# A step of a hybrid transformer layer on one core: x transposed by token tile in the opening, and adaLN slabs in other places

## The chip, the core and the metric

The kernel runs on one core of one Trainium2 chip. A core has TensorE (PE; its weight loads are shown apart as PEld), VectorE (DVE), ScalarE (ACT), GpSimd (POOL) and SyncE (SP), which issues most of the transfers from DRAM. The metric is the device time of one execution in microseconds (us), the median of several runs.

## The reference

One layer of a flow-matching backbone on 384 tokens (128 context tokens, 256 latent ones), width 2048, all in float32. What bears on the change is its beginning:

```python
mod = silu(cond) @ ada_w + ada_b          # cond: c_ctx for the context, c for the latents; 6 parts of 2048
h = rmsnorm(x, norm_w[0]) * (1 + scale_a) + shift_a
proj = h @ w_in                           # q, k, v, o, gates, u
```

Of `mod` the first two parts, shift and scale (i = 0 and 1 in the kernel), are needed for h. Behind it come a bidirectional mLSTM over 8 heads, a pooling mixer on u, an output projection and a squared-ReLU MLP of width 8192; they are the greater part of the time and the change leaves them alone.

## The kernel before, in words

Float32 products are made of three matmuls: an operand is split into `hi` (ACT rounds it to fp32r) and `lo` (DVE subtracts), and hi*hi + lo*hi + hi*lo is summed in PSUM. `load_w` (L119 to L136) fetches a block of weights to `raw` (three buffers) and splits it so.

The opening has four threads. **x**: three token tiles `x_tok` of 128 x 2048 are loaded; ACT sums their squares (L389) for the RMS norm's rstd `rx`, which a matmul spreads over all partitions (`bc_rx`, copied to `rbc`). `transpose_x(k)` (L400) takes the k-th 128 columns of all three token tiles into one PSUM bank and copies them, 128 x 384 at a time, to `xT[k]`; even k on DVE, odd k on ACT. **adaLN**: the columns of `ada_w` for one pair of k tiles come in slabs of 512 KB (four for shift, four for scale), and four matmuls a slab (L257, eight in the profile, since each is recorded twice) sum them in a bank. `ada_rows` copies that bank to SBUF (`ada_sb`, ACT, L269), turns it with small matmuls (L273), and `ada_finish` (L281, L286) writes `mod`. **h**: `make_h(s)` (L437) makes h for one pair of k tiles: `hm` = xT * scale * rbc on DVE (four operations, L443), `hh` = hi of hm + shift on ACT (L448), `hl` on DVE (L449). **Weights** of u and v, in five chunks per k pair: u 0, u 512, v 0, v 3 and v 6 (with the gates); written below as u, u_512, v0, v3, v6.

`X_ORDER` sets by letters how transposes (t), adaLN steps (a) and the row of rstd (b) follow each other. The main loop (L491) then goes over eight k pairs and five chunks, with three token tiles each; between chunks it takes steps of the adaLN generator `ada0` for the next pair: in the first pair by `ADA_STEPS`, after that by a fixed rule. `load_ahead` issues the weights of coming chunks. In the first part the order on PE, DVE and ACT is as written; in the main loop PE's is as written, and a scheduler set that of DVE and ACT ahead of time. All three run strictly in their order, as does SP's queue.

Slabs go into four buffers of their own (`adap`, tag ada) and into four spare places: the second halves of the three x tiles, which are u's tiles later, and the masks (`spare`, L433).

## Time and profile before

| | us |
|---|---|
| median of 3 runs | 1685.16 |
| the runs | 1682.71 to 1686.5 |
| the profiled execution | 1684.17 |
| its span | 1682.5 |
| PE busy in the span | 1654.3 (98%) |
| DVE busy | 1340.3 (80%) |
| ACT busy | 751.3 (45%) |

Times in the views count from the start of the span. In a timeline row stand start, length, engine, line, operation, out<-in, shape and count, and in brackets the idle time before it and what ended it. In the chain of waits stand start, length and what the end of the program waited for in that time. In a row by stretch stand the stretch and its length, then for PE, PEld, DVE, ACT and POOL the busy time and the number of instructions, then the granted clock of PE, the busy share of the DMA engines and GB/s. PE's matmuls overlap: their records are longer than the distance from one start to the next.

### The profile page before, as it was taken

Reading aid. Unit: us, or ns where it says so; the run is one execution under the profiler, and the core shown is the slowest. Engines: PE = TensorE matmul, PEld = TensorE weight load, DVE = VectorE, ACT = ScalarE, POOL = GpSimd, SP = SyncE. Lnnn points to the kernel's source line nnn. Section 1 sums busy time; section 2 is a strip of 40 time slices with the busy share of each in tenths; the row PEclk is TensorE's granted clock in tenths of the full one; section 3 lists DMA queues with packets and bytes.
Section 4 is the critical chain, followed back from the end, with each engine's and each line's share of the span. In section 5 each row is a group of like instructions: output and inputs, shape, how many; then the busy total and the mean of one; then the engine's idle time right before and its main releaser. Section 6 shows DMA issues by size and latency. Waiting matters only on the chain.

```text
span 1682.5 us, 27870 instructions
## 1 busy us (share of the span) xinstructions
PE 1654.3 (98%) x10965; PEld 1581.4 (94%) x10965; DVE 1340.3 (80%) x2009; ACT 751.3 (45%) x1225; POOL 133.3 (8%) x185
## 2 busy tenths in 40 slices
PE   6999999999999999999999999999999999999997
PEld 3888999999999989989999999999999999999996
DVE  3677769898999959997897688988588588588688
ACT  5322355555443345543444444444444444445443
POOL 1000002221000024520000000000000000000120
PEclk9999999999999999999999999999999999999999
DMA  9999757786789954754546246444344443443653
GB/s 318 332 310 298 253 172 248 240 258 221 238 273 311 311 194 142 209 151 128 178 154 195 84 135 187 152 144 150 101 151 129 123 138 118 145 124 113 186 182 136
DMA packets 258099, 320.95 MB, mean 191 GB/s; under 512 B 14784, under 2 KB 223120, under 8 KB 257584
## 3 DMA queue, kind: packets, MB, share of 16 engines
q1 hardware_dynamic: 250688, 303.62, 57.1%
q0 software_dynamic: 5984, 13.78, 2.9%
q8 instruction: 86, 1.41, 0.4%
q10 hardware_dynamic: 1296, 1.77, 0.3%
q14 instruction: 45, 0.37, 0.1%
HBM read 308.61 MB, written 10.51 MB: 190 GB/s over the span
## 4 chain that ended last, share of the span: by engine, by line
PE 94%; DVE 3%; issue 1%; DMA 1%; ACT 0%; SPq 0%; POOL 0%; DVEq 0%; ACTq 0%; POOLq 0%
PE acc_w L145 10%; PE acc_w L144 10%; PE acc_w L146 10%; PE v L503 4%; PE y L1231 4%; PE y L1232 4%; PE y L1230 4%; PE u L503 4%; PE acc_wo L144 3%; PE acc_wo L145 3%; PE acc_wo L146 2%; PE y_yz L1231 2%; PE y_yz L1230 2%; PE y_yz L1232 2%; PE y L1074 2%; PE y L1073 2%
## 5 line engine op out<-in xcount | busy, mean ns | idle before, releaser
L145 PE MATMUL acc_w<-h2l,hi_w 128*128 128x384 f32 (+1 forms) x1024 | 346.2, 338 | 0.5 <-DVE h2l L1024 0.5
L144 PE MATMUL acc_w<-h2h,hi_w 128*128 128x384 f32 (+1 forms) x1024 | 344.2, 338 | 1.2 <-ACT h2h L1020 1.2
L146 PE MATMUL acc_w<-h2h,lo_w 128*128 128x384 f32 (+1 forms) x1024 | 345.1, 337 | 0.0
L136 DVE TENSOR_TENSOR lo_w<-raw_w,hi_w 128x1024 fp32r<-128x1024 f32 x152 | 185.3, 1220 | 136.5 <-ACT hi_w L135 136.3
L135 ACT ACTIVATE hi_w<-raw_w 128x1024 fp32r<-128x1024 f32 x152 | 160.8, 1058 | 213.7 <-PE acc_w L145 83.4
L317 DVE SCALAR_TENSOR_TENSOR ada_acc<-ada_raw,sg,ada_acc 128x1024 f32<-128x1024 f32 (+1 forms) x240 | 252.0, 1081 | 2.1 <-DMA ada_raw<-in_ada_w_dram 2.1
L144 PEld LDWEIGHTS acc_w<-h2h,hi_w 128*128 128x128 f32 x1024 | 192.2, 188 | 2.9 <-ACT h2h L1020 2.0
L145 PEld LDWEIGHTS acc_w<-h2l,hi_w 128*128 128x128 f32 x1024 | 192.6, 188 | 1.2 <-DVE h2l L1024 0.8
L146 PEld LDWEIGHTS acc_w<-h2h,lo_w 128*128 128x128 f32 x1024 | 192.4, 188 | 0.3 <-DVE lo_w L136 0.2
L1216 ACT ACTIVATE hi_t<-w 128x1024 fp32r<-128x1024 f32 x104 | 109.5, 1059 | 118.7 <-PE y L1232 34.0
L1217 DVE TENSOR_TENSOR lo_t<-w,hi_t 128x1024 fp32r<-128x1024 f32 x104 | 126.3, 1220 | 15.1 <-ACT hi_t L1216 14.7
L1217 DVE TENSOR_TENSOR lo_b<-w,hi_b 128x1024 fp32r<-128x1024 f32 x78 | 95.3, 1221 | 40.0 <-ACT hi_b L1216 39.8
L1216 ACT ACTIVATE hi_b<-w 128x1024 fp32r<-128x1024 f32 x78 | 82.5, 1060 | 97.0 <-PE acc_w L145 64.6
L135 ACT ACTIVATE hi_wo<-raw_wo 128x1024 fp32r<-128x1024 f32 x32 | 34.0, 1064 | 81.3 <-DMA raw_wo<-in_w_out_dram 64.0
L950 ACT ACTIVATE z<-acc_w 128x384 f32<-128x384 f32 x54 | 26.3, 487 | 74.8 <-PE acc_w L146 74.8
L503 PE MATMUL v<-hi_v,hh 128*128 128x384 f32 (+1 forms) x144 | 47.8, 332 | 0.0
L503 PE MATMUL v<-lo_v,hh 128*128 128x384 f32 (+1 forms) x144 | 46.5, 323 | 0.0
L503 PE MATMUL v<-hi_v,hl 128*128 128x384 f32 (+1 forms) x144 | 46.5, 323 | 0.0
L136 DVE TENSOR_TENSOR lo_wo<-raw_wo,hi_wo 128x1024 fp32r<-128x1024 f32 x32 | 38.8, 1218 | 7.3 <-ACT hi_wo L135 6.3
L986 POOL DMA_DIRECT2D gf_dram<-gfT x1 | 0.5, 521 | 551.9 <-DVE gfT L985 551.9
L144 PE MATMUL acc_k<-hh,hi_k 128*128 128x384 f32 x128 | 44.2, 345 | 0.0
L144 PE MATMUL acc_o<-hh,hi_o 128*128 128x384 f32 x128 | 43.9, 343 | 0.0
(2268 smaller groups left out, 4566.9 us busy)
## 6 DMA issues: line engine op xcount, KB each, us to landing
raw_w<-in_w_dram SPq DMA_DIRECT2D x152, 512.0 KB, 4.3
ada_raw<-in_ada_w_dram SPq DMA_DIRECT2D x130, 512.0 KB, 5.0
w<-in_w_dram SPq DMA_DIRECT2D x104, 512.0 KB, 4.4
raw_wo<-in_w_out_dram SPq DMA_DIRECT2D x32, 512.0 KB, 5.6
u<-in_ada_w_dram SPq DMA_DIRECT2D x18, 512.0 KB, 6.0
raw_u<-in_w_in_dram SPq DMA_DIRECT2D x16, 512.0 KB, 7.0
raw_q<-in_w_in_dram SPq DMA_DIRECT2D x16, 512.0 KB, 4.7
raw_k<-in_w_in_dram SPq DMA_DIRECT2D x16, 512.0 KB, 4.7
```

The costliest lines, as they stand in the source:

```text
L135: nc.scalar.activation(hi[:, 0:n], raw[:, 0:n], AF.Copy)
L136: low = lambda: nc.vector.tensor_tensor(lo[:, 0:n], raw[:, 0:n], hi[:, 0:n].bitcast(F32), op=ALU.subtract)
L144: nc.tensor.matmul(ps, lh, rh, start=start, stop=False)
L145: nc.tensor.matmul(ps, lh, rl, start=False, stop=False)
L146: mm3.ins = nc.tensor.matmul(ps, ll, rh, start=False, stop=stop).ins
L317: nc.vector.scalar_tensor_tensor(acc[:, g, :], raw[:, a, :], cj, acc[:, g, :], op0=ALU.mult, op1=ALU.add)
L503: nc.tensor.matmul(acc[i][:, 0:n], h[k0 + k][a][:, i * P:(i + 1) * P], (hi, lo)[b][:, k, :], start=k == 0 and a + b == 0, stop=k == nk - 1 ...
L1216: nc.scalar.activation(hi, raw, AF.Copy)
L1217: nc.vector.tensor_tensor(lo, raw, hi.bitcast(F32), op=ALU.subtract)
L1230: nc.tensor.matmul(acc, xh, wh, start=start and j == 0, stop=False)
L1231: nc.tensor.matmul(acc, xh, wl, start=False, stop=False)
L1232: nc.tensor.matmul(acc, xl, wh, start=False, stop=stop and j == 3)
```

## The change

x is transposed by token tile. `transpose_x(i, k0, on_act)` takes four k tiles of one token tile into a bank, and the copies are 128 x 128, four a bank, on DVE or ACT by a flag; all `xT` tiles are allocated ahead. x_prompt is the first load on SP; the constants are loaded from ACT's queue. Two banks of the context tile and one bank of each latent tile are transposed as the tiles land; a list `x_rest` of eight more banks is worked off at the x's of the new `X_ORDER` and in `shift_rows`, so that no transposes are left behind u. u's first weights are loaded in two halves (one per k tile) with a rounding each, `hi_first`, which `make_h(0)` calls ahead of each k tile's hh.

In the first k pair `ADA_STEPS` moves the adaLN steps: the first four slabs from behind u to behind u_512, the second four from behind v0 to behind v3. These second four now go into the spare places, and in the later pairs the first four slabs use the `adap` buffers and the last four the spare ones. The small matmuls and `make_h(1)` move from the middle of v3 into v6, behind its first three matmuls. `AHEAD` sets how far weights are issued ahead in the first pair.

```diff
@@ -28,9 +28,9 @@
 N_E = 1
-XT_AT = 0
-ADA_STEPS = (4, 0, 4, 0, 0)
-X_ORDER = "tatatatattaatabata"
+ADA_STEPS = (0, 4, 0, 4, 0)
+AHEAD = (1, 1, 3, 2, 3)
+X_ORDER = "aaxabaxaaxaxaxax"
 N_X = 4
@@ -77,15 +77,16 @@
     masks = vp.tile([P, N_CST - 3, P], F32, name="masks")
-    nc.sync.dma_start(cc[:, 0, :], c_ctx.rearrange("(p j) -> p j", j=16))
-    nc.sync.dma_start(cc[:, 1, :], c[0].rearrange("(p j) -> p j", j=16))
-    nc.sync.dma_start(cst[:, 0:3], cs_src[:, 0:3])
+    nc.scalar.dma_start(cst[:, 0:3], cs_src[:, 0:3])
...
     x_tok = [pre.tile([P, D], F32, tag=f"x{i}", name=f"xtok{i}") for i in range(3)]
-    for t, src in zip(x_tok, (x_prompt[0], x_sample[0, 0:128], x_sample[0, 128:256])):
-        nc.sync.dma_start(t, src)
+    nc.sync.dma_start(x_tok[0], x_prompt[0])
+    nc.sync.dma_start(cc[:, 0, :], c_ctx.rearrange("(p j) -> p j", j=16))
+    nc.sync.dma_start(cc[:, 1, :], c[0].rearrange("(p j) -> p j", j=16))
+    for i in (1, 2):
+        nc.sync.dma_start(x_tok[i], x_sample[0, (i - 1) * P:i * P])
     nc.gpsimd.dma_start(prm[0:96, 1, :], ada_b[0].rearrange("(r p) -> r p", p=P))
@@ -237,7 +238,7 @@
-    def ada_mat(parts, tags=("ada",), raws=None):
+    def ada_mat(parts, tags=("ada",), raws=None, into=()):
@@ -249,7 +250,8 @@
                 if raw is None:
-                    raw = (wp if tag == "lo" else adap).tile([P, nj, w], F32, tag=tag, name=f"ada_raw_{i}_{k0}_{j0}", bufs=N_W if tag == "lo" else N_ADA)
+                    raw = (into[b][j0 // nj] if into else
+                           (wp if tag == "lo" else adap).tile([P, nj, w], F32, tag=tag, name=f"ada_raw_{i}_{k0}_{j0}", bufs=N_W if tag == "lo" else N_ADA))
                     nc.sync.dma_start(raw, aw[:, j0:j0 + nj, c0:c0 + w])
@@ -348,7 +350,8 @@
             elif k0 == 2:
-                yield from ada_mat([(0, k0, nk), (1, k0, nk)])
+                some = [adap.tile([P, 4, 256], F32, tag="ada", name=f"ada_raw_0_{k0}_{j}", bufs=N_ADA) for j in range(0, 16, 4)]
+                yield from ada_mat([(0, k0, nk), (1, k0, nk)], into=(some, spare))
             else:
@@ -359,9 +362,9 @@
                 i, j0 = divmod(4 * len(raws), 16)
-                raw = (spare.pop(0) if len(raws) < 4 else
+                raw = (spare.pop(0) if len(raws) >= 4 else
                        adap.tile([P, 4, 256], F32, tag="ada", name=f"ada_raw_{i}_{k0}_{j0}", bufs=N_ADA))
-                if len(raws) < 4:
+                if len(raws) >= 4:
                     spare.append(raw)
@@ -375,51 +378,59 @@
     ada0 = first_ada()
+    ssq = const.tile([P, 3, 2], F32, name="ssq")
+    junk = wp.tile([P, 1024], F32, tag="hi", name="junk", bufs=N_W)
+    rx = const.tile([P, 3], F32, name="rx")
+    ss = const.tile([P, 3], F32, name="ss")
+    xT_dram = dram.tile([P, KT, NTOK], F32, name="xT_dram")
+    xT = [slot(f"xT{k}") for k in range(KT)]
+    rbc = pre.tile([P, NTOK], F32, name="rbc")
+    def squares(i):
+        for q in range(2):
+            nc.scalar.activation(junk, x_tok[i][:, q * 1024:(q + 1) * 1024], AF.Square, accum_out=ssq[:, i, q:q + 1])
+    xt_late = []
+    def transpose_x(i, k0, on_act, later=False):
+        ps = bank(f"xt_{i}_{k0}")
+        for a in range(4):
+            nc.tensor.transpose(ps[:, a * P:(a + 1) * P], x_tok[i][:, (k0 + a) * P:(k0 + a + 1) * P], ident)
+        def copy():
+            for a in range(4):
+                dst, src = xT[k0 + a][:, i * P:(i + 1) * P], ps[:, a * P:(a + 1) * P]
+                if on_act:
+                    nc.scalar.activation(dst, src, AF.Copy)
+                else:
+                    nc.vector.tensor_copy(dst, src)
+        if later:
+            xt_late.append(copy)
+        else:
+            copy()
+    squares(0)
+    for q in range(2):
+        transpose_x(0, 4 * q, False)
     pp = bank("pp")
...
     nc.vector.tensor_copy(prmT[:, 0:80], pp[:, 96:176])
-    ssq = const.tile([P, 3, 2], F32, name="ssq")
-    junk = wp.tile([P, 1024], F32, tag="hi", name="junk", bufs=N_W)
-    rx = const.tile([P, 3], F32, name="rx")
-    for i in (0, 1, 2):
-        for q in range(2):
-            nc.scalar.activation(junk, x_tok[i][:, q * 1024:(q + 1) * 1024], AF.Square, accum_out=ssq[:, i, q:q + 1])
-    xT_dram = dram.tile([P, KT, NTOK], F32, name="xT_dram")
-    xT = []
-    rbc = pre.tile([P, NTOK], F32, name="rbc")
-    ss = const.tile([P, 3], F32, name="ss")
+    squares(1)
+    transpose_x(1, 0, False)
+    squares(2)
+    transpose_x(2, 0, False)
     nc.vector.tensor_reduce(ss, ssq, axis=AX.X, op=ALU.add)
     rstd_cols(rx, ss, 3, 1.0 / D)
-    xt_late = []
-    def transpose_x(k, later=False):
-        ps = bank(f"xt_{k}")
-        for i in range(3):
-            nc.tensor.transpose(ps[:, i * P:(i + 1) * P], x_tok[i][:, k * P:(k + 1) * P], ident)
-        t = slot(f"xT{k}")
-        xT.append(t)
-        def copy():
-            if k % 2:
-                nc.scalar.activation(t[:, 0:NTOK], ps[:, 0:NTOK], AF.Copy)
-            else:
-                nc.vector.tensor_copy(t[:, 0:NTOK], ps[:, 0:NTOK])
-        if later:
-            xt_late.append(copy)
-        else:
-            copy()
+    x_rest = [(1, 4, False), (1, 8, True), (1, 12, True), (2, 4, False), (2, 8, False), (2, 12, False), (0, 8, False, True), (0, 12, True, True)]
     for op in X_ORDER:
-        if op == "t":
-            transpose_x(len(xT))
-        elif op == "a":
+        if op == "a":
             next(ada0)
+        elif op == "x":
+            transpose_x(*x_rest.pop(0))
         else:
@@ -443,7 +454,9 @@
             between()
-        for k, t, hi, lo in ts:
+        for n, (k, t, hi, lo) in enumerate(ts):
+            if s == 0:
+                hi_first[n]()
             for g, (a, b) in enumerate(GROUPS):
@@ -462,8 +475,12 @@
-    lo_later = []
-    loaded = {0: load_chunk(0, 0, later=lo_later)}
+    raw0 = wp.tile([P, 2, 512], F32, tag="raw", name="raw_u_first", bufs=3)
+    hi0, lo0 = (wp.tile([P, 2, 512], F32R, tag=t, name=f"{t}_u_first", bufs=N_W) for t in ("hi", "lo"))
+    for k in range(2):
+        nc.sync.dma_start(raw0[:, k, :], wv_in[:, k, U0:U0 + 512])
+    hi_first = [lambda k=k: nc.scalar.activation(hi0[:, k, :], raw0[:, k, :], AF.Copy) for k in range(2)]
+    loaded = {0: (hi0, lo0, 512)}
@@ -475,14 +492,12 @@
     def shift_rows():
-        for _ in range(2):
-            transpose_x(len(xT), True)
         next(ada0)
-        for _ in range(2):
-            transpose_x(len(xT), True)
+        while x_rest:
+            transpose_x(*x_rest.pop(0))
     h_ins = make_h(0, shift_rows)
-    lo_later[0]()
+    nc.vector.tensor_tensor(lo0, raw0, hi0.bitcast(F32), op=ALU.subtract)
     for copy in xt_late:
@@ -491,7 +506,7 @@
             k0, nk = ksteps[s]
-            load_ahead(5 * s + ci, 1 if s + ci == 0 else N_AHEAD)
+            load_ahead(5 * s + ci, AHEAD[ci] if s == 0 else N_AHEAD)
             hi, lo, n = loaded.pop(5 * s + ci)
@@ -502,16 +517,17 @@
                                              start=k == 0 and a + b == 0, stop=k == nk - 1 and b == 1)
-                    if ci == 3 and k == 0:
+                        if s == i == k == 0 and ci == 4:
+                            with tc.high_priority():
+                                next(ada0)
+                                make_h(1)
+                    if s > 0 and ci == 3 and k == 0:
                         next(ada0, None)
...
                 load_ahead(1, 1)
-            if s == 0 and ci == XT_AT:
-                while len(xT) < KT:
-                    transpose_x(len(xT))
             for _ in range((ADA_STEPS if s == 0 else (1, 1, 1, 0, 0))[ci]):
                 next(ada0, None)
-            if ci == 3 and s < NS - 1:
+            if ci == 3 and 0 < s < NS - 1:
                 make_h(s + 1)
...
```

Names below carry the program's buffer numbers; the lines are those of the kernel before, and of the changed one.

DVE ahead of u's first matmuls, before (xT6 is a transposed k tile, `mod` in L281 the shift):

```order
L411 COPY xT6_217<-xt_6_213 128x384
L207 TENSOR_TENSOR dg_rx_225<-cst_72,rx_126 128x384
L424 COPY rbc_134<-bc_rx_227 128x384
L443 SCALAR_TENSOR_TENSOR hm0_261<-xT0_143,mod_118,rbc_134 128x128
L443 SCALAR_TENSOR_TENSOR hm0_261<-xT0_143,mod_118,rbc_134 128x256
L443 SCALAR_TENSOR_TENSOR hm1_266<-xT1_156,mod_118,rbc_134 128x128
L443 SCALAR_TENSOR_TENSOR hm1_266<-xT1_156,mod_118,rbc_134 128x256
L281 TENSOR_TENSOR mod_118<-ada_0_0_206,prmT_117 128x4
L449 SCALAR_TENSOR_TENSOR hl0_263<-hm0_261,mod_118,hh0_262 128x128
```

The same place in the changed kernel:

```order
L406 COPY xT12_136<-xt_2_12_299 128x128
L406 COPY xT13_137<-xt_2_12_299 128x128
L406 COPY xT14_138<-xt_2_12_299 128x128
L406 COPY xT15_139<-xt_2_12_299 128x128
L454 SCALAR_TENSOR_TENSOR hm0_319<-xT0_124,mod_118,rbc_140 128x128
L454 SCALAR_TENSOR_TENSOR hm0_319<-xT0_124,mod_118,rbc_140 128x256
L454 SCALAR_TENSOR_TENSOR hm1_324<-xT1_125,mod_118,rbc_140 128x128
L454 SCALAR_TENSOR_TENSOR hm1_324<-xT1_125,mod_118,rbc_140 128x256
L283 TENSOR_TENSOR mod_118<-ada_0_0_245,prmT_117 128x4
L462 SCALAR_TENSOR_TENSOR hl0_321<-hm0_319,mod_118,hh0_320 128x128
```

The four copies of token tile 2's last bank now stand ahead of hm; the rstd row's operations stand further up.

PE at the end of the first k pair, before:

```order
L257 MATMUL ada_0_2_361<-ada_raw_1_2_8_465,cT_109 32x256 x4
L257 MATMUL ada_0_2_361<-ada_raw_1_2_12_471,cT_109 32x256 x4
L503 MATMUL v_3_0_0_488<-hi_v_3_0_397,hh0_262 128x384
L503 MATMUL v_3_0_0_488<-hi_v_3_0_397,hl0_263 128x384
L503 MATMUL v_3_0_0_488<-lo_v_3_0_398,hh0_262 128x384
L503 MATMUL v_3_0_1_489<-hi_v_3_0_397,hh0_262 128x384
L503 MATMUL v_3_0_1_489<-hi_v_3_0_397,hl0_263 128x384
L503 MATMUL v_3_0_1_489<-lo_v_3_0_398,hh0_262 128x384
L503 MATMUL v_3_0_2_490<-hi_v_3_0_397,hh0_262 128x384
L503 MATMUL v_3_0_2_490<-hi_v_3_0_397,hl0_263 128x384
L503 MATMUL v_3_0_2_490<-lo_v_3_0_398,hh0_262 128x384
L273 MATMUL ada_0_2_361<-cst_72,ada_sb_0_2_477 128x4 x2
```

and in the change, where the slabs lie in u's tiles and the masks:

```order
L518 MATMUL v_3_0_2_488<-hi_v_3_0_451,hl1_326 128x384
L518 MATMUL v_3_0_2_488<-lo_v_3_0_452,hh1_325 128x384
L259 MATMUL ada_0_2_419<-u0_308,cT_109 32x256 x4
L259 MATMUL ada_0_2_419<-u1_309,cT_109 32x256 x4
L259 MATMUL ada_0_2_419<-u2_310,cT_109 32x256 x4
L259 MATMUL ada_0_2_419<-masks_81,cT_109 32x256 x4
L518 MATMUL v_6_0_0_544<-hi_v_6_0_458,hh0_320 128x288
L518 MATMUL v_6_0_0_544<-hi_v_6_0_458,hl0_321 128x288
L518 MATMUL v_6_0_0_544<-lo_v_6_0_459,hh0_320 128x288
L275 MATMUL ada_0_2_419<-cst_72,ada_sb_0_2_527 128x4 x2
L518 MATMUL v_6_0_1_545<-hi_v_6_0_458,hh0_320 128x288
```

The second four slabs' matmuls moved from ahead of v3 to behind it, and the small matmuls from the middle of v3 to the fourth place in v6.

ACT at the same place, before:

```order
L269 ACTIVATE ada_sb_0_2_477<-ada_0_2_361 128x256
L135 ACTIVATE hi_u_0_1_484<-raw_u_0_1_482 128x1024
L522 ACTIVATE v0_85<-v_3_0_0_488 128x3x128
L135 ACTIVATE hi_u_512_1_537<-raw_u_512_1_535 128x1024
L522 ACTIVATE v1_86<-v_3_0_1_489 128x3x128
L448 ACTIVATE hh2_515<-hm2_514,mod_118 128x128
L448 ACTIVATE hh2_515<-hm2_514,mod_118 128x256
L448 ACTIVATE hh3_520<-hm3_519,mod_118 128x128
L448 ACTIVATE hh3_520<-hm3_519,mod_118 128x256
L522 ACTIVATE v2_87<-v_3_0_2_490 128x3x128
L522 ACTIVATE v0_85<-v_6_0_0_541 128x2x128
L522 ACTIVATE v1_86<-v_6_0_1_542 128x2x128
```

and in the change:

```order
L136 ACTIVATE hi_u_0_1_534<-raw_u_0_1_532 128x1024
L538 ACTIVATE v2_85<-v_3_0_2_488 128x3x128
L136 ACTIVATE hi_u_512_1_540<-raw_u_512_1_538 128x1024
L271 ACTIVATE ada_sb_0_2_527<-ada_0_2_419 128x256
L136 ACTIVATE hi_v_0_1_596<-raw_v_0_1_594 128x768
L538 ACTIVATE v0_83<-v_6_0_0_544 128x2x128
L538 ACTIVATE v1_84<-v_6_0_1_545 128x2x128
L538 ACTIVATE v2_85<-v_6_0_2_546 128x2x128
L461 ACTIVATE hh2_556<-hm2_555,mod_118 128x128
L461 ACTIVATE hh2_556<-hm2_555,mod_118 128x256
```

`ada_sb` stood ahead of both roundings of u's next weights and now stands behind both, and the copies of v6 moved from behind hh to ahead of it.

## The prediction

> **What bounds the kernel now.** I read the page first, then the busy times by stretch, the chain of waits over the opening, and the timelines of VectorE (DVE) and ScalarE (ACT) at the two places where the order changes. The page and the stretches:
>
> ```profile
> span 1682.5 us, 27870 instructions
> PE 1654.3 (98%) x10965; PEld 1581.4 (94%) x10965; DVE 1340.3 (80%) x2009; ACT 751.3 (45%) x1225; POOL 133.3 (8%) x185
> ...
> 16.20:29.84 13.64, 12.93 (x108) 6.51 (x108) 5.40 (x16) 5.04 (x11) 0.89 (x1) 1.00 1.09 356
> 29.84:53.21 23.37, 23.37 (x171) 19.21 (x172) 12.24 (x25) 15.39 (x30) 0.00 (x0) 1.00 1.02 334
> ...
> 53.21:400.00 346.79, 346.79 (x2345) 317.78 (x2344) 278.74 (x524) 151.67 (x339) 36.41 (x36) 1.00 0.81 259
> ```
>
> From 29.84, when u's first matmul starts, TensorE (PE) is busy in every microsecond to 400 (second column against the first). So a microsecond won or lost on PE before that stays to the end, and the question is only when PE gets through the opening. The opening itself is paced by the stream from DRAM, 350 GB/s at a DMA share of 1.0. The chain of waits there (start, us, what):
>
> ```profile
> 3.61 12.58 DMA ada_raw<-in_ada_w_dram
> ...
> 16.32 1.08 PE ada L257 x8
> ...
> 19.25 0.83 PE xt L403 x3
> 20.08 0.94 PE ada L257 x8
> 21.02 0.48 PE xt L403 x3
> 21.50 0.57 PE ada L257 x8
> ...
> 25.38 0.91 PE bc_rx L209 x2
> ...
> 28.03 0.39 ACT ada_sb L269
> 28.42 0.95 ACT hi_u L135
> ...
> 29.39 0.41 ACT hh L448
> ...
> 29.84 4.61 PE u L503 x18
> 34.45 1.31 PE xt L403 x12
> 35.76 1.86 PE ada L257 x32
> 37.62 4.38 PE u L503 x18
> 42.01 3.16 PE v L503 x18
> 45.17 1.87 PE ada L257 x32
> 47.03 1.78 PE v L503 x9
> 48.82 0.34 PE ada L273 x4
> 49.16 4.05 PE v L503 x27
> 53.21 8.32 PE u L503 x36
> ```
>
> The first adaLN slab lands at 3.61 + 12.58 = 16.2. At 349 GB/s a 512 KB slab takes 1.50 us, so the eighth lands at 26.7 and u's weights at 28.2; ACT then splits them (0.95), makes h (0.41), and u starts. PE runs at half rate at first: eight adaLN matmuls (four steps) cost 0.94 until 21.0 and 0.57 after, three transposes 0.83 and 0.48.
>
> **Term 1, the opening.** SyncE (SP) issues x_prompt first instead of fourth:
>
> ```profile
> 0.81 0.38 SPq L80 DMA_DIRECT2D cc<-in_c_ctx_dram  x1
> 1.24 0.42 SPq L81 DMA_DIRECT2D cc<-in_c_dram  x1
> 1.71 0.42 SPq L82 DMA_DIRECT2D cst<-in_consts_dram  x1
> 2.18 0.43 SPq L88 DMA_DIRECT2D xtok<-in_x_prompt_dram  x1
> ```
>
> The stream's start moves by at most 2.18 - 0.81 = 1.37 us and at least by the one issue that leaves SP (0.47). The bytes stay. I take 1.2, since little moves in the first 2 us now: slabs at 15.0, 16.5, ... 25.5, u's two halves at 26.2 and 27.0. By the Trainium skill (Trainium Kernel Development and Optimization, Key Constraints), issues from several engines share the same 16 DMA engines and save only issue time. By that rule alone the constants on ACT's queue are worth one issue, 0.47; this sum does not rest on it. c now stands behind 1 MB of x in SP's queue, but is wanted only at the first slab, 15.0.
>
> No PE work is removed: 48 transposes before and after, 36 before u until now, all 48 in the change, so 1.31 us leaves the place behind u. The copies change more. Sixteen copies of 384 columns become 48 of 128, and 36 of these on DVE. Their rows, with the h operations:
>
> ```profile
> 9.26 0.26 DVE L381 COPY prmT<-pp 128x96 f32<-128x96 f32 x1 [3.45 <-PE pp L380]
> 9.44 0.23 DVE L382 COPY prmT<-pp 128x80 f32<-128x80 f32 x1
> 24.30 0.56 DVE L411 COPY xT<-xt 128x384 f32<-128x384 f32 x1 [0.62 <-PE xt L403]
> 24.78 0.55 DVE L207 TENSOR_TENSOR dg_rx<-cst,rx 128x384 f32<-128x384 f32 x1
> 26.92 1.41 DVE L443 SCALAR_TENSOR_TENSOR hm<-xT,mod,rbc 128x128 f32<-128x128 f32 x4
> 29.19 0.16 DVE L281 TENSOR_TENSOR mod<-ada,prmT 128x4 f32<-128x4 f32 x1 [0.86 <-PE ada L273]
> ```
>
> A 128-column copy lies between 0.26 (96 columns) and 0.56 (384); small copies start 0.18 apart. Four in a row: between 0.8 and 2.0, and I take 0.9, near the 96-column row. All but one bank's copies lie beside PE. That one counts: in the new order the last bank of the middle transposes (token tile 2, k 12 to 15) is copied on DVE right ahead of hm, and hm stands ahead of the shift's mod. Today hm runs at 26.92, under the last slabs' matmuls.
>
> PE, step by step: slab one 15.0 to 16.0 and two 16.5 to 17.5 at half rate, a bank of four transposes (4/3 x 0.83 = 1.1) to 18.6, slab three to 19.6. The rstd row bc_rx waits for those transposes' copies (0.9) and dg_rx (0.55): 18.6 + 1.45 = 20.1, and runs 0.91 to 21.0. Then at full rate five slabs (5 x 0.6), five banks of transposes (5 x 0.65) and the small matmuls (0.34), 6.6 us, to 27.6. PE is the late one, as slab eight is wanted at 26.3 and there at 25.5. Behind 27.6: copies 0.9, hm 1.41, mod 0.2, first hh 0.41, passing on 0.1: u starts at 30.6, against 29.84. u's 18 matmuls take 4.9 instead of 4.61, because ACT splits the second half of the weights (about 0.5) between the two k tiles' hh. They end at 35.5, where u and its transposes now end at 35.76. Splitting the weights in two takes the 0.95 of hi_u off the chain, but the copies and hm stand there instead. Term 1: **-0.3 us**. Bounds: if PE is never behind the stream, u starts at 25.5 + 0.57 + 0.65 + 3.0 = 29.7 and the term is -1.2; if half rate lasts until 23, +0.8.
>
> **Term 2, the step to the second k pair.** The second four slabs of k pair 1 move from ahead of the chunk v3 to behind it. The small matmuls that finish mod move from the middle of v3 into v6, and make_h(1) with them. Rows of ACT and DVE today at this place:
>
> ```profile
> 50.21 1.05 ACT L135 ACTIVATE hi_u<-raw_u 128x1024 fp32r<-128x1024 f32 x1
> 51.16 0.49 ACT L522 ACTIVATE v<-v 128x384 f32<-128x384 f32 x1
> 51.53 1.49 ACT L448 ACTIVATE hh<-hm,mod 128x128 fp32r<-128x128 f32 x4
> ...
> 49.61 1.23 DVE L136 TENSOR_TENSOR lo_u<-raw_u,hi_u 128x1024 fp32r<-128x1024 f32 x1
> ...
> L136 DVE TENSOR_TENSOR lo_v<-raw_v,hi_v 128x768 fp32r<-128x768 f32 x4 | 3.7, 954 | 2.3 <-ACT hi_v L135 2.3
> ```
>
> Count from v3's start. PE: v3 3.16, adaLN 1.86, three matmuls of v6 (0.137 each) 0.41: free for the small matmuls at 5.43. ACT in its new order: v3's second token tile is done after 15 of 18 matmuls, 2.8; then the copy (0.37 to the next start, 51.16 to 51.53), hi_u (0.95, 50.21 to 51.16), the copy of tile three (0.37), hi_u of the second half (0.95): 5.45. Only then ada_sb, 0.39, and PE goes on at 5.9: **0.5** lost. Today nine matmuls of v3 (1.6 us) cover ada_sb.
>
> The small matmuls end at 6.25 and the 15 left of v6 at 8.3: only 2.0 us cover make_h, against 4.05 today. On DVE stand, in order, lo_u of the second half (1.23, to 6.75), mod, lo_v (0.95), the rest of mod, to 8.0, then gsb, which waits for v6's first tile and its copy (7.9), then hm: its first piece is ready at 8.5. ACT copies v6's last tile at 8.4 to 8.8, then the first hh: 9.15, so u of k pair 1 starts at 9.2 instead of 8.3: **0.9** lost. Its second matmul wants hl, which stands behind all four hm (1.41): 9.8 instead of 9.4: **0.4**. Term 2: **+1.8 us**, between +0.5 (ada_sb alone) and +2.5.
>
> The transfers of this stretch are covered: the four slabs in the halves of x's tiles land by about 45.5 and are wanted at 44.9 + 3.16 = 48.1: they are issued behind v6's weights at about 37, and from issue to landing pass at least 4.0 us, and then 1.5 each:
>
> ```profile
> DMA to landing us min/median/max: 4.0/8.9/15.2
> ```
>
> From the next k pair on, PE, DVE and ACT have the old order, but for slabs first into their own places and then into the spare ones.
>
> **Sum.** -0.3 + 1.8 = +1.5 us on the profiled execution's 1684.17 (span 1682.5 and 1.67 around it): 1685.7. The runs' median is 1685.16, 0.99 above the profiled one, within their 1682.71 to 1686.5; on the median the sum gives 1686.7. I take the middle, **1686.2**.
>
> **Rivals.** (a) PE reaches full rate earlier: x_prompt's eight transposes at about 5.5 to 7.7 and the next banks keep PE busier than today's one transpose at a time. If it is at full rate from slab one, the ledger ends 0.8 earlier, u starts at 29.8 and the whole is +0.7: 1685.4. The Trainium skill (TensorE: Matmul & The Clock Gate, Part 1) says PE runs at half rate until about 3.4 us of sustained work and again after an idle window as long. The trace agrees in the size, full rate 4.7 us after the slabs' matmuls begin at 16.3; whether the gaps between x's tiles count as idle no row shows.
>
> (b) Faster: the covers work as the order means them, so that the last bank's copies and hm fit before the shift's mod. Then u starts at 25.5 + 0.57 (slab) + 0.5 (ada_sb) + 0.34 + 0.2 + 0.41 + 0.1 = 27.6, u ends at 32.3, -3.5, and with make_h(1) hidden but ada_sb's 0.5 paid it is -3.0; with 1.37 instead of 1.2 of stream and ada_sb hidden, -3.7: 1681.5. Against it: DVE's order, in which hm cannot pass the copies.
>
> (c) Slower: on ACT, hi_u of the second half stands ahead of ada_sb, and waits for its weights. They are the sixth transfer behind v6's weights, which SP issues when DVE has made lo_u (about 36): 37 + 4.0 + 5 x 1.5 = 48.5. v3 starts at 35.5 + 4.38 + 1.86 + 3.16 = 44.9, so they are wanted at 49.4. From 0.9 us late this decides; 3 us late, say by slabs waiting for their places, it adds 2.1 to 1.5, with PE idle behind ada_sb: +3.6 on the sum's base of 1685.2, about 1689.
>
> **How the numbers follow.** Less than 0.2% (3.4 us) cannot be told from no change here. Forecast 0.55 and (a) 0.15 fall within it: 0.70. (b) 0.15 is faster, (c) 0.15 slower. The range runs from 1682.0, near (b), to 1689.0, at (c): the terms' bounds give -0.7 to +3.3 about either base, and the runs' own spread of 3.8 us is added.
>
> **What would show it.** Right: u's first matmul at 30 to 31 with hh and hm, not hi_u, ahead of it in the chain; copies of xT from 128 columns just ahead of hm; PE idle before the small matmuls in v6 (on ACT ada_sb) and before u of k pair 1 (on ACT hh, DVE hl), 1.8 together. Wrong: u's first matmul before 29, no idle PE between 36 and 60, or PE waiting for a DMA there.

## The result, and the profile after the change

The changed kernel takes **1691.3 us** (median of 8 runs, 1687.0 to 1693.62) against 1684.81 for the kernel before (8 runs, 1682.71 to 1686.98). The ratio is 1.0034, with a 95% interval from 1.0023 to 1.0046: slower by 5.7 us. The forecast was 1686.2 and no change, with a range to 1689.0. It was wrong.

The profiled execution of the changed kernel took 1693.62, the slowest of its eight, and its span is 9.4 us longer than the one before. From the page:

```profile
span 1691.9 us, 27901 instructions
PE 1665.4 (98%) x10965; PEld 1588.7 (94%) x10965; DVE 1343.5 (79%) x2037; ACT 749.7 (44%) x1230; POOL 133.0 (8%) x185
```

Busy times by stretch, from the first slab's matmuls to u, from there to u of k pair 1, and on to 400:

```profile
15.37:33.81 18.44, 16.39 (x106) 7.99 (x107) 7.05 (x31) 4.16 (x15) 0.88 (x1) 1.00 1.09 354
33.81:59.04 25.23, 24.24 (x158) 18.75 (x158) 12.10 (x24) 15.56 (x33) 0.00 (x0) 0.93 0.83 267
59.04:400.00 340.96, 340.73 (x2299) 311.33 (x2300) 271.38 (x517) 147.99 (x330) 34.89 (x36) 1.00 0.81 256
```

The bound was read rightly: behind the opening PE is busy without a break, so what it loses there stays. But the opening takes 18.4 us from the first slab to u in place of 13.5 (16.32 to 29.84). The chain of waits of the changed kernel shows the stretch piece by piece (start, us, what):

```profile
18.96 0.88 DVE xT L406 x4
19.84 0.47 DVE dg_rx L208
...
20.36 1.65 PE bc_rx L210 x2
22.01 1.01 PE ada L259 x8
23.02 1.05 PE xt L398 x4
24.07 0.65 PE ada L275 x4
...
27.78 0.93 PE xt L398 x4
28.71 0.57 PE ada L259 x8
...
31.05 0.88 DVE xT L406 x4
31.94 1.31 DVE hm L454 x4
33.25 0.08 DVE mod L283
...
33.35 0.80 ACT hh L461 x2
...
46.48 6.00 PE v L518 x33
...
59.76 8.39 PE u L518 x35
```

Eight adaLN matmuls cost 1.01 us until 27.8 and 0.57 from 28.7: half rate lasted to about 28.4, where the kernel before left it at about 20.8. The rest is as the forecast drew it: the copies of the last bank (0.88), hm (1.31), mod and hh stand ahead of u. Behind the first slabs and bc_rx, PE's timeline has three waits over 0.2 us as far as u of k pair 1, one ahead of u's first matmul and two at u of k pair 1 (in brackets):

```profile
33.81 2.83 PE L518 MATMUL u<-hi_u_first,hh 128*128 128x512 f32 x6 [1.28 <-ACT hh L461]
...
59.04 0.49 PE L518 MATMUL u<-hi_u,hh 128*128 128x512 f32 x1 [0.76 <-ACT hh L461]
59.76 0.50 PE L518 MATMUL u<-hi_u,hl 128*128 128x512 f32 x1 [0.23 <-DVE hl L462]
```

Against the kernel before, the chain of waits reaches v 4.5 us late (46.48 against 42.01), and u of k pair 1 6.6 us (59.76 against 53.21). So in this profile the opening cost 4.5 and the step to the second k pair 2.1. The last 2.8 of the 9.4 came at 547, among the matmuls of the output projection (`acc_wo`), in a place that the change does not touch; an experiment below deals with it. As this execution was the slowest of eight, its losses are larger than those of most runs.

The grant of PE's clock changes only at points 3.41 us apart (in every profile of this study). Cut along these points, the windows of the opening before and after are as follows (PE's busy time is the number behind the window's length; the clock column shows nothing of the half rate ahead of the first grant, which has to be read from the durations). Before, up to the full rate at 20.83:

```profile
14.00:17.42 3.42, 1.57 (x10) 0.50 (x11) 0.25 (x3) 2.95 (x6) 0.00 (x0) 1.00 1.08 358
17.42:20.83 3.41, 3.41 (x22) 1.32 (x22) 1.09 (x3) 0.49 (x1) 0.89 (x1) 1.00 1.10 349
```

After, up to the full rate at 28.45 and on to the end of u's first matmuls:

```profile
14.80:18.21 3.41, 2.58 (x19) 0.84 (x19) 1.21 (x6) 1.40 (x4) 0.88 (x1) 1.00 1.09 348
18.21:21.62 3.41, 2.98 (x14) 1.01 (x12) 1.35 (x5) 0.00 (x0) 0.00 (x0) 1.00 1.10 348
21.62:25.04 3.42, 3.42 (x21) 2.08 (x24) 0.74 (x3) 1.17 (x5) 0.00 (x0) 1.00 1.10 355
25.04:28.45 3.41, 3.41 (x24) 1.64 (x16) 0.14 (x1) 0.78 (x4) 0.00 (x0) 1.00 1.06 372
...
31.86:35.28 3.42, 2.05 (x11) 1.11 (x8) 2.58 (x9) 1.93 (x6) 0.00 (x0) 1.00 0.75 249
35.28:38.69 3.41, 3.41 (x9) 2.59 (x9) 3.33 (x8) 1.68 (x6) 0.00 (x0) 0.50 0.12 19
```

Before, the first window that PE filled with slabs and transposes brought the full rate. After, the window at 18.21 has a hole of 0.43 us (bc_rx waits for dg_rx, which stands on DVE behind four copies of xT), and the window at 21.62 holds the first small matmuls (0.65 us, two columns wide, at 24.07). Only the window behind both counted. And when PE then waited 1.3 us for hh, the window behind that ran at half rate again, just under u's first matmuls. This became the theory to test: **full rate comes with the first window of a fixed grid that PE fills, and the new order breaks up its work so that, where the grid lay here, no window was filled before 25**. That the small matmuls do not count is so far a guess from one window. Its rivals: the loss lies in the copies and the later hm, or at the second k pair.

### The profile page after: what moved, and what is told of

It reads as the page before. It is cut to its first block, busy times and chain, and to the rows that moved or that the text cites. A ratio compares the mean times of both kernels' runs of the same rounds, so it can differ in the third digit from the quotient of the medians.

```text
span 1691.9 us, 27901 instructions
## 1 busy us (share of the span) xinstructions
PE 1665.4 (98%) x10965; PEld 1588.7 (94%) x10965; DVE 1343.5 (79%) x2037; ACT 749.7 (44%) x1230; POOL 133.0 (8%) x185
## 4 chain that ended last, share of the span: by engine, by line
PE 89%; DVE 6%; DMA 2%; issue 2%; ACT 1%; SPq 0%; POOL 0%; DVEq 0%; ACTq 0%; POOLq 0%
PE acc_w L146 10%; PE acc_w L145 10%; PE acc_w L147 10%; PE v L518 4%; PE u L518 4%; PE y L1247 4%; PE y L1248 4%; PE y L1246 4%; PE acc_wo L145 2%; PE acc_wo L146 2%; PE acc_wo L147 2%; PE y_yz L1246 2%; PE y_yz L1247 2%; PE y_yz L1248 2%; PE y L1088 2%
## 5 line engine op out<-in xcount | busy, mean ns | idle before, releaser
L145 PE MATMUL acc_q<-hh,hi_q 128*128 128x384 f32 x128 | 43.9, 343 | 0.0
```

Source lines behind the costliest of these rows:

```text
L145: nc.tensor.matmul(ps, lh, rh, start=start, stop=False)
```

## The experiments

All were timed in five rounds beside the kernel before; ratios are to it. A gain or loss in us beside a ratio is worked out from the ratio; it need not equal the difference of the two medians, and half the width of the 95% intervals is 1.4 to 1.9 us.

### Which half of the change costs

The opening alone (the boundary of the first k pair as before the change):

```diff
-ADA_STEPS = (0, 4, 0, 4, 0)
+ADA_STEPS = (0, 4, 4, 0, 0)
-                        if s == i == k == 0 and ci == 4:
-                            with tc.high_priority():
-                                next(ada0)
-                                make_h(1)
-                    if s > 0 and ci == 3 and k == 0:
+                    if ci == 3 and k == 0:
...
-            if ci == 3 and 0 < s < NS - 1:
+            if ci == 3 and s < NS - 1:
```

> The changed opening with the old order at the end of the first k pair (second four slabs between v0 and v3, small matmuls in the middle of v3, make_h(1) behind v3). Theory: the change costs about 6 us, of which 2.1 at the end of the first k pair (PE idle there before the small matmuls and before u of k pair 1) and the rest in the opening, where PE stays at half rate until 28.5 and falls back to it at 35.3. Then this kernel is 2 us faster than the change and still 3.5 to 4.5 us slower than before, and u of k pair 1 starts about 57.5 in the profile. Rival: the slow opening is an accident of one profiled run and the order at the end of the k pair is the whole loss: then it is within 1 us of before.

Measured: 1687.87 against 1685.97, ratio 1.0016 (1.0006 to 1.0026): +2.7 us, where 3.5 to 4.5 were expected. Its profiled execution (1692.13, the slowest of twelve) had the full rate at 28.42 as the change had, so most runs lose less in the opening than the two profiles show.

The boundary alone, put into the kernel before:

```diff
-ADA_STEPS = (4, 0, 4, 0, 0)
+ADA_STEPS = (4, 0, 0, 4, 0)
-                    if ci == 3 and k == 0:
+                        if s == i == k == 0 and ci == 4:
+                            with tc.high_priority():
+                                next(ada0)
+                                make_h(1)
+                    if s > 0 and ci == 3 and k == 0:
...
-            if ci == 3 and s < NS - 1:
+            if ci == 3 and 0 < s < NS - 1:
```

> The old opening with the new order at the end of the first k pair alone (second four slabs behind v3, small matmuls and make_h(1) in v6; the slabs keep their places). Theory: 1.5 to 2.5 us slower than before, PE idle before the small matmuls (0.5) and before u of k pair 1 (1.3), with ACT's hh and DVE's hl named. Rival, in which the loss comes mostly from here: 4 us or more slower. Rival, in which the new opening brings these waits about: no change.

Measured: 1688.84 against 1685.97, ratio 1.0021 (1.0012 to 1.0030): +3.5 us, where 1.5 to 2.5 were expected. The two add up to 6.2, near the change's 5.7. In this kernel the order on ACT decides, and a transfer decides over ACT; its timeline:

```profile
50.70 1.06 ACT L135 ACTIVATE hi_u<-raw_u 128x1024 fp32r<-128x1024 f32 x1 [1.88 <-DMA raw_u<-in_w_in_dram]
...
51.66 0.37 ACT L269 ACTIVATE ada_sb<-ada 128x256 f32<-128x256 f32 x1
...
52.08 0.61 PE L273 MATMUL ada<-cst,ada_sb 128*128 128x4 f32 x4 [1.33 <-ACT ada_sb L269]
```

hi_u of the next pair's second half waits for its weights, ada_sb stands behind it, and PE waits 1.33 us. That is rival (c) of the prediction, in a milder form, and in the old opening; in the changed kernel itself the weights came in time: ACT's timeline has no wait for a DMA there.

### Full rate by extra work, and hm taken forward

The changed kernel with 16 more transposes of x, whose results nothing reads, ahead of the second and third token tiles and the first slab:

```diff
+    def filler(n, tok):
+        if n:
+            ps = bank(f"fill_{tok}")
+            for a in range(n):
+                nc.tensor.transpose(ps[:, (a % 4) * P:(a % 4 + 1) * P], x_tok[0][:, a * P:(a + 1) * P], ident)
...
+    filler(8, 'x1')
     transpose_x(1, 0, False)
+    filler(6, 'x2')
     transpose_x(2, 0, False)
+    filler(2, 'ada')
```

> The change, with 16 more transposes of x_prompt into banks that nobody reads: 8 ahead of the second token tile's first bank, 6 ahead of the third's, 2 ahead of the first slab, where PE waits for transfers. Theory of the clock: with PE busy from 7 us on it reaches full rate by 14 to 18 instead of 28.5, the slabs' matmuls take 0.57 a four from then on, u starts at 30.5 to 31 instead of 33.8, and the whole is 2.5 to 4 us faster than the change. Rival of the copies: u's start is set by DVE's copies and hm and by the stream, the extra transposes bring nothing or cost up to 1 us. Rival: the rate depends on work from one moment of the clock's own, and full rate comes as late as before the extra work.

Measured: 1690.24 against 1685.97, ratio 1.0026 (1.0017 to 1.0035). The rate was full at 13.2, half again from 16.6 to 20.0, behind a window in which PE waited 0.72 for a bank and 0.78 for a slab, and full from there on. u's first matmul came at 30.18 in place of 33.81. It still waited for hh:

```profile
30.18 2.34 PE L527 MATMUL u<-hi_u_first,hh 128*128 128x512 f32 x6 [1.28 <-ACT hh L470]
```

So in this profile the late rate is worth up to 3.6 us in the opening (the first slab was 0.25 us earlier too), and PE's wait behind the rival's copies and hm is 1.3 at u's start with the early rate as with the late one. The end of the run gained less than u's start. In the profile, u of k pair 1 was 4.5 us earlier than in the changed kernel and the end 3.2. By the ratios the runs are only some 1.4 us faster than the change, less than the 2.5 to 4 expected, and the two intervals overlap.

The changed kernel with hm of the first pair ahead of the second slabs (DVE makes it as soon as the scale is there):

```diff
-X_ORDER = "aaxabaxaaxaxaxax"
+X_ORDER = "aaxabaxaaxhaxaxax"
+        elif op == "h":
+            first_ts = scaled(0)
...
-        ts = []
+        ts = first_ts if s == 0 else scaled(s)
```

Here `scaled(s)` holds the hm operations that stood in `make_h(s)`.

> The change, with hm of the first k pair (four DVE operations) ahead of the last three banks' copies on DVE instead of behind them. Theory of the order on DVE: hm's 1.3 us leave the chain, u starts 1.3 earlier as far as PE has done its transposes by then (about 32.5 at half rate), and the whole is 1 to 1.5 us faster than the change. Rival: PE at half rate is what sets u's start, and the gain is under 0.5 us.

Measured: 1689.33 against 1685.97, ratio 1.0021 (1.0012 to 1.0031), some 2 us less than the change (1 to 1.5 expected; the intervals overlap), with the 1.28 us ahead of u gone. What hm alone is worth this profile cannot tell, as the rate came earlier too: it was full from 24.76, because the grid lay so that one window (21.35 to 24.76) fitted between the start of bc_rx and the first of the small matmuls. In the changed kernel the same small matmuls fell inside the window.

Both repairs, hm early and the old boundary:

> This kernel takes both repairs together: hm of the first two strips ahead of the second slabs (as in the kernel with hm early) and the boundary of the first k pair as before the change (ada_sb, hm and hh2 placed as there). If the two losses add, as the opening alone (+2.7 us) and the boundary alone (+3.5 us) added up to the change's 5.7: the boundary's 3.5 is gone and hm early takes some 2 of the opening's 2.7, so +0.5 us against the kernel before (ratio 1.0003, between 0.9995 and 1.0010), u's first matmul at 31 to 32.5, u of the second k pair near 53. If the boundary's cost came from the new opening (transfers later there): +2 us or more, with PE idle ahead of the small matmuls at 50 to 52.

Measured: 1686.29 against 1685.89, ratio 1.0004 (0.9995 to 1.0013), as expected if the losses add.

### The clock by order alone

Three kernels move instructions without adding or removing any. The first takes the last kernel and moves bc_rx from behind the third slab to behind the fourth and two more banks of transposes. One more bank then stands ahead of the first small matmuls, and each later bank stands ahead of a slab that it stood behind:

```diff
-X_ORDER = "aaxabaxaaxhaxaxax"
+X_ORDER = "aaxaaxxbaaxhaxaxa"
```

> The kernel before this one with nothing but the order of the opening changed: bc_rx and two groups of transposes of x stand ahead of the first small matmuls, so that PE has work without a break from the second slab's matmuls (16.8 us) over two slabs, three groups of transposes and bc_rx to about 24.7. No instruction is added or removed. Theory (the full rate comes with the first 3.41 us window that PE fills): the full rate is granted between 20.2 and 23.6 in place of 24.8 to 28.4, u's first matmul at 30 to 30.8, 1 to 2 us less than the kernel before this one (ratio to the kernel before 0.9994). Rival (the rate comes at its own time, or follows the amount of work done, not its continuity): granted at 24.8 or later as before, the same time as the kernel before this one within 0.5 us.

Measured: 1685.12 against 1685.89, ratio 0.9996 (0.9987 to 1.0005), 1.2 us below the kernel that it was made from, which the overlapping intervals do not separate. The rate was full at 19.89 and u's first matmul at 28.69, where the kernel before has 29.84. The window that brought it, 16.48 to 19.89, was busy for 3.08 of 3.41 us: a little earlier than expected, since the wait of 0.34 us for the second slab did not spoil it. In the profile of the kernel with both repairs the rate also came at 19.90, by a window of 3.09 us, so that these two profiles do not tell the orders apart.

The second is the change itself with that string altered:

```diff
-X_ORDER = "aaxabaxaaxaxaxax"
+X_ORDER = "aaxaaxxbaaxaxaxa"
```

> The change itself with one string altered: bc_rx and two groups of transposes go ahead of the first small matmuls, the same instructions in another order; hm stays late and the boundary stays new. Theory (what the change lost in the opening is the late full rate): granted at 19.9 to 23.6 in place of 28.4, u's first matmul near 31 in place of 33.8, 2 to 3 us less than the change: 1688.5 where the kernel before has 1685.9 (ratio 1.0016); what remains is the boundary's 3 us. Rival (the loss lies in the new order's copies and waits): 1.0030 or more as the change had (1.0034).

Measured: **1686.01** against 1685.25, ratio 1.0004 (0.9995 to 1.0013). One string takes back 5 of the 5.7 us, more than the 2 to 3 expected, and its interval lies clear of the change's (1.0023 to 1.0046). Its windows and its chain of waits:

```profile
13.80:17.21 3.41, 2.30 (x16) 1.05 (x20) 1.21 (x6) 2.51 (x6) 0.27 (x1) 1.00 1.09 356
17.21:20.63 3.42, 3.42 (x28) 1.21 (x28) 1.35 (x5) 0.00 (x0) 0.62 (x1) 1.00 1.10 349
```

```profile
26.49 0.89 DVE xT L406 x4
27.38 0.88 DVE hm L454 x3
...
40.44 6.51 PE v L518 x36
...
53.76 7.70 PE u L518 x32
```

The rate was full at 20.63. v's first matmul came at 40.44, 1.6 us ahead of the kernel before, and copies and hm stand in the chain 4.6 us earlier than in the change, in the same order. Not all of that is the rate: the fill, with the change's order and the rate full from 20.0, starts u at 30.18, this kernel at 29.25. That the string also takes away PE's wait of 0.43 us for dg_rx and sets the last bank's transposes ahead of the last slab may be the rest. The new boundary then costs 1.4 (PE waits 0.56 for hl, and by the matmul the lead shrinks from 1.6 to 0.2).

The third goes the other way: it takes the kernel before and sets the four slabs' matmuls one behind the other, with the transposes behind them, so that PE waits 0.4 us for each slab:

```diff
-X_ORDER = "tatatatattaatabata"
+X_ORDER = "taaaatttttaatabata"
```

> The kernel before the change with one string altered: the first four slabs' matmuls stand one behind the other without transposes between them (1.08 us of matmuls, then a wait for the next slab that lands 1.5 us after the last), and five transposed tiles follow them. The same instructions, the same transfers. Theory (a 3.41 us window must be nearly full): PE waits 0.4 us in every 1.5 until 20.7, so that no window before it counts; full rate at 24.1 to 27.5 in place of 20.8, u's first matmul 2 us or more later (32 to 33), ratio 1.0012. Rival (the rate comes with time or with the work done, and PE is paced by the slabs anyway): granted near 20 to 22, u's first matmul by 30.9, ratio 1.0004 or less.

Measured: 1687.34 against 1685.25, ratio 1.0010 (1.0001 to 1.0019). The windows, and PE's timeline on both sides of the full rate:

```profile
18.13:21.55 3.42, 2.57 (x24) 0.40 (x16) 0.00 (x0) 0.00 (x0) 0.15 (x1) 1.00 1.10 349
21.55:24.96 3.41, 3.41 (x21) 3.40 (x17) 1.10 (x2) 1.37 (x3) 0.00 (x0) 1.00 1.10 349
```

```profile
20.55 1.08 PE L257 MATMUL ada<-ada_raw,cT 128*32 128x256 f32 x8 [0.42 <-DMA ada_raw<-in_ada_w_dram]
21.56 3.46 PE L403 MATMUL xt<-cst,xtok 128*128 128x128 f32 x15
24.81 0.58 PE L273 MATMUL ada<-cst,ada_sb 128*128 128x2 f32 x4
25.32 0.64 PE L257 MATMUL ada<-ada_raw,cT 128*32 128x256 f32 x8
...
32.07 1.83 PE L503 MATMUL u<-hi_u,hh 128*128 128x512 f32 x6
```

Full rate at 24.96 and u at 32.07, both inside the expected ranges. So an order that leaves PE idle for a quarter of each window brings the late rate into the old kernel, and an order without holes takes it out of the new one. The rival (the rate comes with time or with the work done) fails in both directions: PE had worked 6.4 us up to the grant in the kernel before, 16.9 in the change, 9.1 with the altered string and 9.6 here.

The position of the grid has its share in this. A window of 3.41 us can be slid over a trace to see where it would hold 3.08 us of PE work, the least that always brought the rate (see the end), small matmuls left out. In the change it may start from 16.5 to 16.8, from 20.0 to 21.0 and from 24.3 on. In the last version below, whose opening has the altered string (with hm early), it may start anywhere from 15.9 to 19.2. By this estimate the rate comes by 24.8 at a third of all positions of the grid in the change's trace (two thirds in that of the opening alone, which has the same order), and by 22.7 at nearly all in the last version's. So the order decides how often the rate is early, and the grid decides in which execution: the kernel with both repairs, in the change's order but for hm, had it at 19.90.

### PE kept busy

28 transposes that nothing uses, added to the kernel with hm early, the old boundary and bc_rx behind:

```diff
-    transpose_x(1, 0, False)
+    transpose_x(1, 0, False, fill=9)
-    transpose_x(2, 0, False)
+    transpose_x(2, 0, False, fill=8)
...
+    fb, fills = bank("fill"), [6, 5]
...
+            for a in range(fills.pop(0) if fills else 0):
+                nc.tensor.transpose(fb[:, (a % 4) * P:(a % 4 + 1) * P], x_tok[0][:, a * P:(a + 1) * P], ident)
```

> The previous kernel with 28 more transposes of x whose results are overwritten or not read (9 ahead of the second token tile, 8 ahead of the third, 6 and 5 ahead of the first two slabs): PE has hardly a wait from 7.7 us on. They leave the output as it is. Theory: full rate from 13 to 14 us on and kept, PE then follows the slabs (last landed at 25.8), small matmuls at 26.8, u's first matmul at 28.3 to 29, u's 18 matmuls done at 33.5 against 35.76 before: 2 us less than the kernel before (ratio 0.9988). Rival (what is lost lies in the copies on DVE and in ACT's hh, not in the rate): no faster than the kernel without the fill, u's first matmul at 30 or later although the rate is full.

Measured: 1687.84 against 1685.89, ratio 1.0014 (1.0006 to 1.0023): slower, where 2 us less were expected. The first half of the theory held: the rate was full from 11.7. But PE was then ahead of the stream, waited 0.96 us for the last slab and 0.57 for ada_sb, and lost the rate as u began:

```profile
25.36:28.77 3.41, 1.88 (x22) 1.16 (x19) 2.12 (x10) 0.90 (x2) 0.00 (x0) 1.00 1.07 369
28.77:32.18 3.41, 3.41 (x13) 3.02 (x13) 2.39 (x6) 3.13 (x10) 0.00 (x0) 0.50 1.09 348
```

u's first matmul came at 30.07. That is 1.4 us behind the same kernel without the extra work (28.69). In this profile the kernel is level with the kernel before at 53 us and loses 2.8 further on; behind 380 PE waits 5.7 us in all where the kernel before waits 3.7, and no run here traces this to a cause.

### The half-rate spell at 547

The kernel before has one wait of PE between 60 and 600:

```profile
PE adaf L336 <- ACT adav_sb L332: 0.7, 1, 0.7
```

adav_sb and the gate's ada_sb share one buffer, so that adav_sb is copied only when the gate's small matmuls are done, and PE waits 0.75 us for it at 540, with small matmuls ahead and behind. In the changed kernel the whole of it fell into one window, and the next two ran at half rate:

```profile
543.86:547.27 3.41, 2.66 (x22) 2.58 (x20) 3.41 (x4) 1.99 (x5) 0.00 (x0) 1.00 1.08 366
547.27:550.69 3.42, 3.42 (x14) 3.42 (x14) 3.42 (x11) 0.25 (x2) 0.00 (x0) 0.50 1.07 373
```

The experiment gives the gate's sums two slots of their own, in the kernel before:

```diff
-        sb = adap.tile([P, 512], F32, tag="adasb", name=f"ada_sb_{parts[0][0]}_{parts[0][1]}", bufs=1)
+        sb = [slot(f"ada_sb_{k}") for k in range(2)] if w == 512 else [adap.tile([P, 512], F32, tag="adasb", name=f"ada_sb_{parts[0][0]}_{parts[0][1]}", bufs=1)]
...
-            nc.scalar.activation(sb[:, 0:w], ps[:, 0:w], AF.Copy)
+            for k, t in enumerate(sb): nc.scalar.activation(t[:, 0:w // len(sb)], ps[:, k * 256:k * 256 + w // len(sb)], AF.Copy)
```

> The kernel before the change with one edit far from the opening: the gate's row sums (ada_sb, 512 columns) go to two slots of 256 columns and no longer share their only buffer with adav_sb, so that adav_sb is copied earlier and PE no longer waits 0.75 us for it at 540 us (the only wait of PE over 0.1 us between 30 and 700 us). The half-rate window that followed this wait in four of the six profiles (at 545.6 to 547.3) was there where the whole wait lay in one window of the 3.41 us grid, and absent where it lay across two. Theory: with the wait goes the window: 0.75 and, in about 3 of 4 executions, 1.7 us: 2.0 us less than the kernel before (ratio 0.9988), and times that lie closer together. Rival (the window has nothing to do with the wait): 0.75 us less at most (0.9996), and a half-rate window near 547 all the same.

Measured: 1684.69 against 1685.89, ratio 0.9990 (0.9981 to 0.9999), with no wait there and no spell. The time does not decide, since the interval holds the rival's 0.9996 as well, nor does this profile, since the kernel before has no spell either. The eleven profiles that still have the wait of 0.75 us do: in six (the change and five of the experiments) the wait and most of the small matmuls behind it lay in one window, and the next was at half rate; in five the grid cut them, and none was. In two of these five the whole wait lay in one window and the cut came behind it, as in the kernel with bc_rx behind, whose grid has a point at 538.72:

```profile
537.00 0.95 PE L275 MATMUL ada_gate<-cst,ada_sb 128*128 128x4 f32 x8
538.69 1.06 PE L338 MATMUL adaf<-cst,adav_sb 128*128 128x4 f32 x8 [0.75 <-ACT adav_sb L334]
```

So the wait alone is not enough. Without the small matmuls, PE's work in the window was 0.97 to 1.44 us in the six, and 1.8 or more in the five. So the profiled execution before, 1684.17, was one of those without the spell, and the one after had a double one.

### Both together

hm early, the old boundary, bc_rx behind, and two slots for the gate's sums:

> The kernel with bc_rx behind the second slabs' transposes (hm early, old boundary) and the gate's row sums in two slots. The two edits touch stretches 500 us apart. If their gains add: 0.8 us (1685.12 against 1685.89) and 1.2 us (1684.69 against 1685.89), together 2.0 us, ratio 0.9988. If the waits only move (a wait saved early is lost again at a transfer later): ratio 0.9992 or more.

Measured: **1682.75** against 1685.25, ratio 0.9984 (0.9975 to 0.9992). This version beats both kernels: 2.5 us less than the kernel before, some 8 less than the change. That the two gains add (2.0 expected) fits; the rival's 0.9992 lies at the interval's edge. In its profile the rate came at 22.63. Its eleven runs lie within 2.4 us (1681.43 to 1683.83), those of the change within 6.6.

## Why the prediction was wrong

**The bound, right for the change.** PE stays busy behind the opening (340.73 of 340.96 us), and the loss stayed. It is not so in every run: in eight of the experiments' profiles PE waits 0.3 to 1.6 us between 300 and 400, in the mLSTM, where the kernels before and after have no wait. One of the eight is the two slots (0.53), whose opening is that of the kernel before. No run here shows what brings these waits; what an experiment gains in the opening can be smaller at the end by as much.

**Term 1, wrong: -0.3 forecast, +4.5 in the profile.** The step that failed is the end of half rate at 21.0, read from the old trace ("PE runs at half rate at first") and carried into the new order as "Then at full rate five slabs", with an upper bound of +0.8 for half rate until 23. The rate came at 28.4, and it was lost again from 35.28 to 38.69, so that u's first 18 matmuls took 6.5 us in place of 4.9 (5.0 in the fill, with the full rate). The forecast took from the old trace the time of the grant, where it should have asked what earned it: a window of 3.41 us that PE filled. The 4.5 is that of the slowest run; by the runs the opening alone costs 2.7, still above the bound of +0.8. Its own ledger contained the hole that broke this stretch, PE waiting for bc_rx, and the small matmuls. The rest of the term held:

- the stream came 0.95 us earlier (first slab's matmuls at 15.37 against 16.32; 1.2 forecast);
- four copies took 0.88 (0.9 forecast), and copies and hm stand ahead of u as drawn;
- the change with bc_rx behind, which has the rate that the forecast assumed (20.6), starts u at 29.25, where 30.6 was forecast, and v 1.6 us early. There term 1 is -1.6, 0.4 beyond the bound of -1.2. That this kernel's median, 1686.01, is near the forecast's 1686.2 is in part luck: its terms are -1.6 and +1.4, not -0.3 and +1.8, and its profile has the spell at 540 besides.

**Rival (a)** weighed the clock but in one direction only, earlier, and the signs of being wrong named a u before 29 but none so late as 33.81. The transposes that it set at 5.5 to 7.7 began at 7.0, when the constants landed: 6.2 us after their issue from ACT's queue, 2.6 after it in the kernel before. The Trainium skill (TensorE: Matmul & The Clock Gate, Part 1) says that the clock gate watches a free-running window of 3413 ns and goes to full rate after one busy window. The grid of 3.41 us in all thirteen profiles agrees, and by that rule the forecast should have laid windows over the new order. How full that window must be is told at the end.

**Term 2, right in size: +1.8 forecast, 2.1 in the change, 1.4 with the early rate.** By the records PE waited 0.13 behind v's start for ada_sb (0.5 forecast), 0.76 for hh (0.9) and 0.23 for hl (0.4), 1.1 in all; the other 1.0 stands as PE busy for longer over the same 91 matmuls, as the two kernels by stretch show (before, then after). Most of that 1.0 is waiting too: a record ends later than the next matmul can start (0.39 long, 0.23 apart for u), which hides part of each wait. Counted from start to start, PE lost 0.3 at the small matmuls, 0.9 at u's first matmul and 0.6 at its second and third, so that the parts too came near the forecast. In the old opening the boundary cost more (+3.5), because there rival (c) came in.

```profile
42.01:53.21 11.20, 11.20 (x91) 10.03 (x91) 3.91 (x12) 6.91 (x14) 0.00 (x0) 1.00 1.03 344
```

```profile
46.48:59.76 13.28, 12.16 (x91) 10.21 (x91) 5.78 (x14) 7.95 (x17) 0.00 (x0) 1.00 1.05 349
```

**Rival (b)**, hm ahead of the shift's mod, needed hm to be written there; with that done and the full rate early, u started at 28.69 (27.6 in the rival). **Rival (c)** did not occur in the change, where the later opening gave the weights time, but in the boundary alone.

**The sum.** The profiled execution before had no spell at 540, so the forecast's correction to the median (+0.99) may have covered something that comes and goes with the grid. It did not decide here. Rival (a) is counted from 1684.7, (b) and (c) from 1685.2; the half microsecond matters nowhere.

## What to carry to other kernels

Where a kernel starts with short pieces of TensorE work, lay a grid of 3.4 us over the new order, in more than one position, and look for a window without holes and without narrow matmuls; the grant's time in the old trace is no property of the machine. When half rate lasts too long, first reorder what is there (here the order in one string was worth 5 us) before adding work: extra work brought u 3.6 us forward in the change, but in the reordered kernel it made PE run into the next transfer, and u came 1.4 us later. A wait of 0.75 us among narrow matmuls, in the middle of dense ones, can cost a window at half rate, 1.7 us, behind it.

## What the runs showed of the hardware

- **How full a window must be.** Over the thirteen profiles, a window of the grid in which PE was busy for 3.08 us or more, not counting the 2-column matmuls, always brought the full rate. Of five with 2.98 or 2.99 us one did (PE kept busy) and four did not, and none below did. Two windows that were full only by counting the small matmuls (3.41 with them, 2.84 and 2.89 without) did not either, nor did one with 4-column matmuls (the change at 547.27: 3.41 with them, 2.56 without).
- **How little takes it away.** A window with 1.81 us (the fill) or 1.88 us (PE kept busy) of PE work was followed by one at half rate, and so was the window at 540 with 0.75 us of waiting and the small matmuls. At 2.05 us it went both ways: lost at u's start in the change, kept in the opening alone. The Trainium skill (TensorE: Matmul & The Clock Gate, Why this matters for your kernels) gives gaps of about 3 us as those to avoid; here waits of 0.75 to 1.5 us within one window were enough in some windows, though not in all, and the measurement decides. No limit separates the two by either count, as the fill kept the rate behind a window with 2.14 us, of which only 1.69 without the small matmuls:

```profile
26.81:30.23 3.42, 2.14 (x17) 1.69 (x17) 2.68 (x12) 1.40 (x4) 0.00 (x0) 1.00 1.07 353
```

- **Scatter.** Where the grid lies against the program changes from one execution to the next (the same opening had the rate at 20.83, 20.73 and 19.63 in the kernel before, the boundary alone and the two slots), and with it whether a window fits between two holes. The change's runs spread over 6.6 us; the last version, with fewer holes, over 2.4. That the grid makes this scatter fits the traces, but with one profile a kernel no run here shows it, and the waits between 300 and 400 come and go as well.
